# A hybrid state-space / RWKV block on one core: buffers and load order at the seam to the recurrence, and state-space steps ordered behind dense sums

## The chip, the cores and the metric

The kernel runs on one core of a Trainium2 chip. The metric is the device time of one execution in microseconds (us). Engines are named as in the profile: PE is TensorE, DVE VectorE, ACT ScalarE, POOL GpSimd, SP SyncE, which here only issues transfers. A core has all five, each with its own queue of instructions that it works off strictly in order.

## The reference, cut to what matters

One layer of a sequence model: 2048 positions, width 1024, all in float32.

```
h = RMSNorm(x);  [u | rwkv_in | gate_a | gate_b] = h @ W_in         # 512 | 1792 | 1024 | 1024 columns
o_a = S5(u):     x_t = A x_(t-1) + B u_t  (complex, diagonal, 32 groups x 64 states);  y = C x + D u;  gelu, half-GLU
o_b = RWKV7(p):  pm = p + (shifted p - p) * mu
                 r, k, v = pm columns;  decay, a from two low-rank products;  g from a third
                 S_t = S_(t-1) * w_t + (S_(t-1) a_t) b_t + v_t k_t ;   y_t = S_t r_t     (8 heads x 64)
merged = sigmoid(gate_a) * (o_a @ Wb_a) + sigmoid(gate_b) * (o_b @ Wb_b)
x = x + merged @ W_out;  x = x + relu(RMSNorm(x) @ W1)^2 @ W2;  out = RMSNorm(x)
```

## The kernel before

The program has four phases, traced one after the other: `phase_a` (norm, input projection, state-space branch), `phase_b` (RWKV recurrence with the gate products in its gaps), `phase_c` (half-GLU, branch and output products) and the feed-forward product. Float32 accuracy comes from splits: each operand is held as a high and a low part, and a product is three matmuls (`mm3`, lines 121 to 123: high weight by low input, low by high, high by high). A *group* is one 128x512 output tile in one PSUM bank: 8 slices of the inner dimension, 24 matmuls.

**The order of instructions** is not the order of the program text. A planner traces the program, simulates it with its own costs, and lets each engine issue what it takes to be ready first, earlier-traced instructions first among those. `tc.keep_in_program_order` (in the code often wrapped as `pin`) binds an instruction behind the one traced just before it on its engine, and only that one. A DMA counts as an instruction of the engine that issues it. Once fixed, each queue is worked off in order, so an instruction that waits holds up all behind it. Generators are woven at trace time: `weave(main, other, ratio=2)` takes two steps of `other` for each `yield` of `main`; `robin` takes one of each in turn.

**Phase A, the dense products** (`dense`, lines 527 to 575). The normalised input lies in SBUF as four tiles of 32 KB per partition: `hh0`, `hl0` (high and low part of windows 0 and 1) and `hh1`, `hl1` (windows 2 and 3). There are 14 weight tiles m in the order 17, 16, 4 ... 15, each with four windows w: 56 groups. After a group ScalarE writes `sg` from the PSUM bank, scaled by `om` (line 557); then VectorE adds the shifted part, the *dense sum* (line 558), adds the column carried from the window before (line 561) and copies the group's last column (line 565). That copy is the last reader of the bank; four banks turn. The tile `sg` (three buffers, shared with the low-rank results) is stored to `pm_d` by SP (line 572). For m = 17, `low_rank` multiplies by small matrices (line 591, two banks at once) and stores the sigmoids (lines 594, 596).

**Phase A, the state-space branch** (`s5_stream`) is woven into the dense groups at ratio 2; `dense` yields twice a group, so four state-space yields fall to one group. The 32 groups are done in 8 passes q. A pass multiplies the input by E (`px`, pinned on TensorE), copies to X, runs 12 *steps* on VectorE (`step`, lines 377 to 383: two multiplications into m1 and m2, two additions), spreads the carries (lines 397 to 403: two multiplications, two additions, for each of two state groups), makes the tables of the next pass (`prep`) and multiplies by F and TZ (`py`, pinned on TensorE). The last pass has no `prep` behind its steps.

**Phase B.** Its pools are opened anew over phase A's memory, and a tile waits for the tiles that lay at its place. From the tile sizes and the order in which the pools are opened: the constants' pool `b_c`, the gate pools `b_w` and `b_t` are stacked at the upper end. The constants `cstb` come first in `b_c` and lie partly over the last 4 KB of `hl1`; the first gate-weight buffer (in `b_w`) lies over the state-space tiles TZ0 and TZ1; the second (in `b_t`) lies over `om` and the last raw weight tile. The recurrence's inputs (pool `b_x`: rm, km, vm, sgx, sig, aa) lie within `hh0`.

The recurrence runs over 16 pieces of 128 positions. `elem(s)` makes the decays and scaled keys of a piece on VectorE, ScalarE and GpSimd (first step line 689, from km), `inv(s)` inverts the in-chunk matrices, `chain(s)` carries the state. At line 1027 `robin` turns between `chain(i-2)`, the gates `gg`, `elem(i)` and `inv(i-1)`. `gates` (from line 957) multiplies the 16 gate-weight tiles by the four windows of h, 64 groups: `raww` loads a raw weight tile, `loadw` splits it (ScalarE cast line 976, GpSimd subtraction line 977) and for the first window stores the split to `gs_d` (line 981). The window's input comes back from `h_d` as eight tiles gh0 to gh7 (`h{k}`): gh0 to gh4 in `b_w`, loaded by GpSimd's queue in the first window, gh5 to gh7 in `b_t`, loaded by SP.

Of the kernel before, what the change touches and what calls it, by code (L numbers as in the profile page):

```python
# [10 lines left out]
F32 = mybir.dt.float32  # L11
F32R = mybir.dt.float32r
# [3 lines left out]
ALU = mybir.AluOpType  # L16
# [5 lines left out]
NK = DM // 128  # L22
# [21 lines left out]
NCST_A = 144  # L44
# [217 lines left out]
def s5_stream(tc, nc, K, io, R, u_d, z_d, pool, ps):  # L262

    NP = 2
    V = nc.vector
# [4 lines left out]
    PW, PR, A8, NI, qr, qi = R.PW, R.PR, R.A8, R.NI, R.qr, R.qi  # L270
# [91 lines left out]
    for q in range(NQ):  # L362
        p0, f0 = q * NP, q * fw
# [10 lines left out]
        m1 = pool.tile([128, 2, NP, 32], F32, tag="m1", name=f"m1{q}")  # L374
        m2 = pool.tile([128, 2, NP, 32], F32, tag="m2", name=f"m2{q}")

        def step(dst, src, k, n):
            shp = [128, 2, NP, n]
            d1, d2 = m1[:, :, :, 0:n], m2[:, :, :, 0:n]
            V.tensor_tensor(d1, src, A8[:, 0:1, k, p0:p0 + NP].unsqueeze(3).to_broadcast(shp), op=ALU.mult)  # L380
            V.tensor_tensor(d2, src[:, ::-1], NI[:, :, k, p0:p0 + NP].unsqueeze(3).to_broadcast(shp), op=ALU.mult)
            V.tensor_tensor(d1, d1, d2, op=ALU.add)
            V.tensor_tensor(dst, dst, d1, op=ALU.add)

# [3 lines left out]
        for j in range(5):  # L388
            n = 32 - (1 << j)
            step(XB[:, :, :, 32 - n:32, 7], XB[:, :, :, 0:n, 7], 7 + j, n)  # L390
            yield
        for g in range(NP):
            shp = [128, 2, 31, 7]
            f1 = pool.tile([128, 2, 31, 7], F32, tag="f1", name=f"f1{q}_{g}")
            f2 = pool.tile([128, 2, 31, 7], F32, tag="f2", name=f"f2{q}_{g}")
            car = XB[:, :, g, 0:31, 7:8]
            V.tensor_tensor(f1, A8[:, 0:1, 0:7, p0 + g].unsqueeze(2).to_broadcast(shp), car.to_broadcast(shp), op=ALU.mult)
            V.tensor_tensor(f2, NI[:, :, 0:7, p0 + g].unsqueeze(2).to_broadcast(shp), car[:, ::-1].to_broadcast(shp),
                            op=ALU.mult)
            yield  # L400
            V.tensor_tensor(f1, f1, f2, op=ALU.add)
            dst = XB[:, :, g, 1:32, 0:7]
            V.tensor_tensor(dst, dst, f1, op=ALU.add)
            yield
# [22 lines left out]
def phase_a(tc, nc, K, io, u_d, pm_d, h_d, z_d):  # L427
    with ExitStack() as st:
# [11 lines left out]
        R = Net()  # L440
# [69 lines left out]
        mu = K.vec("mu_rwkv")  # L510
# [16 lines left out]
        def dense():  # L527
# [4 lines left out]
            for gi, (m, w) in enumerate(groups):  # L532
# [13 lines left out]
                i = m - 4  # L546
                pp = psm.tile([128, 512], F32, tag="mm", name=f"p{m}_{w}")
                o = 512 * (w % 2)
                for k in range(NK):
# [4 lines left out]
                    if side and k in (2, 6):  # L554
                        side.pop(0)()
                sg = wp.tile([128, 512], F32, tag="sg", name=f"sg{m}_{w}", bufs=3)
                nc.scalar.activation(sg, pp, ACTF.Copy, scale=om[:, i:i + 1])
                nc.vector.scalar_tensor_tensor(sg[:, 1:512], pp[:, 0:511], mu[:, i:i + 1], sg[:, 1:512],
                                               op0=ALU.mult, op1=ALU.add)
                if w:  # L560
                    nc.vector.scalar_tensor_tensor(sg[:, 0:1], lasts[m], mu[:, i:i + 1], sg[:, 0:1],
                                                   op0=ALU.mult, op1=ALU.add)
# [48 lines left out]
def phase_b(tc, nc, K, io, pm_d, ob_d, h_d, gt_d, gs_d, inv_d):  # L611
    V, A, P, T = nc.vector, nc.scalar, nc.gpsimd, nc.tensor
    NS = S // 128
    with ExitStack() as st:
# [8 lines left out]
        psi = st.enter_context(tc.tile_pool(name="b_pi", bufs=2, space=PSUM, reuse_waits="tile"))  # L623
        psc = st.enter_context(tc.tile_pool(name="b_pc", bufs=1, space=PSUM, reuse_waits="tile"))
        psy = st.enter_context(tc.tile_pool(name="b_py", bufs=1, space=PSUM, reuse_waits="tile"))
        ct = cp.tile([128, NCST - NCST_A], F32, name="cstb")
        cq = tc.keep_in_program_order(nc.gpsimd.dma_start(ct, io["cst"][:, NCST_A:]))

        def cst(n):
            o, w = COFF[n]  # L630
# [17 lines left out]
        eend = cp.tile([128, 4, 2 * NS + 1], F32, name="eend")  # L648
        gam = cp.tile([128, 4, 2 * NS + 1], F32, name="gam")
        P.memset(eend, 0.0)  # L650
        SB = [cp.tile([128, 4, 128], F32, name=f"SB{i}") for i in range(2)]
        for t in SB:
            P.memset(t, 0.0)

        def gps(n):
            return psg.tile([128, 512], F32, tag="g", name=n)

        D = [dict() for _ in range(NS)]

        def load(s, q=nc.sync):  # L660
            d = D[s]
            for i, n in enumerate(("rm", "km", "vm")):
                d[n] = xp.tile([128, 4, 128], F32, tag=n, name=f"{n}{s}", bufs=3 if n == "vm" else 2)
                (pin(q.dma_start) if s == 0 and n != "vm" else q.dma_start)(d[n], pm_d[512 * i:512 * i + 512, 128 * s:128 * s + 128].rearrange(
                    "(h p) t -> p h t", p=128))
            d["sgx"] = xp.tile([128, 128], F32, tag="sgx", name=f"sgx{s}", bufs=4)
            q.dma_start(d["sgx"], pm_d[1536:1664, 128 * s:128 * s + 128])
            for i, n in enumerate(("sig", "aa")):
                d[n] = xp.tile([128, 4, 128], F32, tag=n, name=f"{n}{s}", bufs=2)
                q.dma_start(d[n], pm_d[1664 + 512 * i:2176 + 512 * i, 128 * s:128 * s + 128].rearrange(  # L670
                    "(h p) t -> p h t", p=128))

        def fl(a):
            return a.rearrange("p h t -> p (h t)")

        def pin(f):
            return lambda *a, **k: tc.keep_in_program_order(f(*a, **k))

        def elem(s):
            d = D[s]  # L680
# [276 lines left out]
        def gates():  # L957
            late, keep = Late(), Late()

            def raww(m, q=nc.sync):  # L960
                wr = (gw, gt)[m % 2].tile([128, NK, 128], F32, tag="wr", name=f"gwr{m}")
                pin(q.dma_start)(wr, io["win"][18 + m])
                return wr

            def loadw(m, wr=None):

                pool = (gw, gt)[m % 2]
                wh = pool.tile([128, NK, 128], F32R, tag="wh", name=f"gwh{m}")
# [7 lines left out]
                A.copy(wh, wr)  # L976
                P.tensor_tensor(wl, wr, wh, op=ALU.subtract)  # L977

                def store():
                    for e, t in enumerate((wh, wl)):  # L980
                        nc.sync.dma_start(gs_d[m, e], t.bitcast(F32))

                keep.put(store)
                return wh, wl

            wr0 = raww(0, nc.gpsimd)
            yield
            wr1 = raww(1)
            for w in range(NW):
                hs = []  # L990
                for k in range(NK):
                    t = (gw if k < 5 else gt).tile([128, 2, 512], F32R, tag=f"h{k}", name=f"gh{w}_{k}")
                    q = nc.sync if w or k >= 5 else nc.gpsimd
                    (q.dma_start if w else pin(q.dma_start))(
                        t.bitcast(F32), h_d[:, w, :, k, :].rearrange("i p t -> p i t"))
                    r = t[:, 0], t[:, 1]
                    hs.append(r)
                if w == 0:
                    nxt = loadw(0, wr0)
                for _ in range(5):  # L1000
                    yield
                for m in range(16):
                    wh, wl = nxt
                    j = 16 * w + m
                    if j == 15:
                        keep.flush()
                    if j + 1 < 16 * NW:
                        nxt = loadw(j + 1, None if j else wr1)
# [10 lines left out]
            late.flush()  # L1019

        gg = Side(gates())
        next(gg)
        load(0, nc.gpsimd)
        next(gg)
        A.copy(bor, bo)
        for i in range(NS + 2):
            robin(chain(i - 2) if i >= 2 else None, gg, elem(i) if i < NS else None,
                  inv(i - 1) if 0 <= i - 1 < NS else None)
# [862 lines left out]
```

## Time and profile before

| what | value |
|---|---|
| median of 3 runs (lowest to highest) | 3067.3 us (3063.57 to 3067.74) |
| the profiled execution's own time | 3067.71 us |
| span in that profile, first to last instruction | 3065.8 us |
| mean granted TensorE clock | 0.975 |
| TensorE busy | 2915.4 us, 95% |
| VectorE busy | 1897.8 us, 62% |
| ScalarE busy | 1121.4 us, 37% |
| GpSimd busy | 1234.7 us, 40% |
| last dense matmul issued; dense products end | 539.97 us |
| first gate matmul | 550.17 us |

A row of the instructions in order of time reads: start in us, duration in us, engine, line, operation, output <- inputs, shapes, count; in brackets the idle time of the engine before it and what ended it. SPq is SP's queue. In the stretches each engine has its busy time and instruction count, then come the granted clock (1.00 is full), the DMA engines' busy share and GB/s. In the rows of DMA issues the last number is the median time from issue to landing.

### The profile page before, as it was taken

To read this page: it belongs to the slowest core of one execution; us is meant where nothing else is said; L and a number is where in the kernel's file an instruction comes from. 1 tells how busy PE (TensorE), PEld (TensorE's weight loads), DVE (VectorE), ACT (ScalarE), POOL (GpSimd) and SP (SyncE) were. 2 spreads that over 40 slices of the span, in tenths; PEclk is the share of its full clock that TensorE was granted. 3 is DMA by queue.
4 is the path that set the end of the run, shared out by engine and by line. 5 is a ranking of instruction groups with operands and counts; after the bars stand their busy time and mean duration, and the time that the engine had idled before them with its cause. 6 is when DMAs were issued, how large, how long until landed. Compare 5 with 4: busy or idle time off the path is not lost.

```text
span 3065.8 us, 45565 instructions
## 1 busy us (share of the span) xinstructions
PE 2915.4 (95%) x17024; PEld 2329.5 (76%) x17024; DVE 1897.8 (62%) x3307; ACT 1121.4 (37%) x1797; POOL 1234.7 (40%) x1082
## 2 busy tenths in 40 slices
PE   8989999689999999999999989999999999999998
PEld 6757777467777777777878778887788788888886
DVE  6366885467777677535322376658655476666667
ACT  5342111234333333234444365555433432222232
POOL 3101101754443343113333345555544565555563
PEclk9999999789999999999999999999999999999999
DMA  4344444755656455367665653333533486666664
GB/s 154 96 132 148 132 148 133 255 187 176 187 167 207 120 149 181 118 195 229 194 213 166 192 188 124 110 110 114 169 113 107 134 240 151 151 151 151 153 146 148
DMA packets 328172, 486.04 MB, mean 159 GB/s; under 512 B 112832, under 2 KB 171712, under 8 KB 327952
## 3 DMA queue, kind: packets, MB, share of 16 engines
q1 hardware_dynamic: 298352, 438.08, 44.8%
q0 software_dynamic: 12960, 40.87, 7.3%
q10 hardware_dynamic: 16640, 4.20, 0.5%
q8 instruction: 134, 2.20, 0.3%
q14 instruction: 86, 0.70, 0.1%
HBM read 327.71 MB, written 147.85 MB: 155 GB/s over the span
## 4 chain that ended last, share of the span: by engine, by line
PE 55%; DVE 10%; DMA 6%; issue 4%; POOL 3%; ACT 2%; SPq 1%; POOLq 0%; DVEq 0%; ACTq 0%
PE s L121 6%; PE s L122 6%; PE s L123 6%; PE f L121 6%; PE f L123 6%; PE f L122 6%; PE gp L121 2%; PE gp L122 2%; PE gp L123 2%; DMA g<-gt_d 1%; PE o L121 1%; DVE yt L813 1%; PE o L122 1%; DVE YC L815 1%; PE o L123 1%
## 5 line engine op out<-in xcount | busy, mean ns | idle before, releaser
L121 PE MATMUL f<-bl,w1h 128*128 128x512 f32 x896 | 354.4, 396 | 9.4 <-ACT w1h L1378 9.3
L122 PE MATMUL f<-bh,w1l 128*128 128x512 f32 x896 | 350.7, 391 | 5.1 <-POOL w1l L1382 5.1
L123 PE MATMUL f<-bh,w1h 128*128 128x512 f32 x896 | 352.1, 393 | 0.0
L121 PE MATMUL s<-w2l,ah 128*128 128x512 f32 x784 | 305.8, 390 | 2.9 <-ACT s L1619 2.9
L122 PE MATMUL s<-w2h,al 128*128 128x512 f32 x784 | 305.7, 390 | 0.0
L123 PE MATMUL s<-w2h,ah 128*128 128x512 f32 x784 | 305.6, 390 | 0.0
L1382 POOL TENSOR_TENSOR w1l<-w1r,w1h 128x512 fp32r<-128x512 f32 x122 | 179.9, 1478 | 180.2 <-ACT w1h L1378 179.8
L121 PE MATMUL gp<-gh,gwh 128*128 128x512 f32 x512 | 225.8, 441 | 21.4 <-ACT gwh L976 14.9
L122 PE MATMUL gp<-gh,gwl 128*128 128x512 f32 x512 | 211.6, 413 | 12.5 <-POOL gwl L977 11.7
L1378 ACT CAST w1h<-w1r 128x512 fp32r<-128x512 f32 x224 | 137.9, 620 | 207.9 <-PE f L123 149.7
L1596 POOL TENSOR_TENSOR al<-ra,ah 128x1024 fp32r<-128x1024 f32 x64 | 168.4, 2634 | 109.2 <-ACT ah L1595 109.0
L123 PE MATMUL gp<-gh,gwh 128*128 128x512 f32 x512 | 209.3, 409 | 0.0
L1626 DVE TENSOR_TENSOR c<-c,s 128x512 f32<-128x512 f32 x224 | 149.9, 684 | 90.5 <-PE s L123 89.8
L121 PEld LDWEIGHTS f<-bl,w1h 128*128 128x128 f32 x896 | 169.4, 189 | 45.7 <-ACT w1h L1378 10.9
L122 PEld LDWEIGHTS f<-bh,w1l 128*128 128x128 f32 x896 | 169.1, 189 | 44.6 <-POOL w1l L1382 7.9
L123 PEld LDWEIGHTS f<-bh,w1h 128*128 128x128 f32 x896 | 168.9, 188 | 38.3
L121 PE MATMUL p<-hl,wh 128*128 128x512 f32 x448 | 183.1, 409 | 0.2
L122 PE MATMUL p<-hh,wl 128*128 128x512 f32 x448 | 178.7, 399 | 0.0
L123 PE MATMUL p<-hh,wh 128*128 128x512 f32 x448 | 178.2, 398 | 0.0
L121 PEld LDWEIGHTS s<-w2l,ah 128*128 128x128 f32 x784 | 147.5, 188 | 33.9 <-ACT s L1619 3.3
L123 PEld LDWEIGHTS s<-w2h,ah 128*128 128x128 f32 x784 | 147.6, 188 | 30.9
L122 PEld LDWEIGHTS s<-w2h,al 128*128 128x128 f32 x784 | 147.5, 188 | 30.6
(392 smaller groups left out, 6778.7 us busy)
## 6 DMA issues: line engine op xcount, KB each, us to landing
w1r<-in_w_dram SPq DMA_DIRECT2D x64, 512.0 KB, 3.5
r_d<-c SPq DMA_DIRECT2D x128, 256.0 KB, 2.0
ra<-r_d SPq DMA_DIRECT2D x64, 512.0 KB, 3.5
gwl<-gs_d SPq DMA_DIRECT2D x48, 512.0 KB, 4.5
gwh<-gs_d SPq DMA_DIRECT2D x48, 512.0 KB, 4.8
ch<-r_d POOLq DMA_DIRECT2D x42, 512.0 KB, 5.7
gt_d<-gs SPq DMA_DIRECT2D x64, 256.0 KB, 5.0
g<-gt_d SPq DMA_DIRECT2D x64, 256.0 KB, 3.4
```

The costliest lines, as they stand in the source:

```text
L121: nc.tensor.matmul(ps, wh, xl, start=start, stop=False)
L122: nc.tensor.matmul(ps, wl, xh, start=False, stop=False)
L123: nc.tensor.matmul(ps, wh, xh, start=False, stop=stop)
L813: V.tensor_tensor(tv, NC[:, 0:k, k:k + 1].to_broadcast([64, k, n]), YC[:, k:k + 1, k:16].to_broadcast([64, k, n]), op=ALU.mult)
L815: V.tensor_tensor(YC[:, 0:k, k:16], YC[:, 0:k, k:16], tv, op=ALU.add)
L1378: cast = A.copy(h, o)
L1382: (P if n % 2 or edge else V).tensor_tensor(l, o, h, op=ALU.subtract)
L1596: P.tensor_tensor(l, raw[n], h, op=ALU.subtract)
L1626: V.tensor_tensor(d, d, bank, op=ALU.add if i in (4, 5, 6) else ALU.subtract)
```

## The change

Five edits, none of which changes what is computed.

1. In `s5_stream`, the two multiplications of every step and of every carry block are bound behind the latest dense sum that was traced before them (`R.last`, line 558); `tc.issue_after` adds an order on VectorE and no wait for completion. The multiplications into f1 and f2 (lines 397 and 398) are wrapped in the same way as those of `step`.
2. In `b_c`, the two state buffers SB are made first and the constants after them, so that the constants lie 4 KB higher. SB's memsets are traced later, just before the loop.
3. Both raw gate-weight buffers are now in `b_w` (tags wr0 and wr1). In exchange gh4 moves from `b_w` to `b_t`, to the place over `om`, and from GpSimd's queue to SP's.
4. The first loads are pinned in a new order, all on GpSimd's queue: gate weights 0, constants, then km, sig, aa, rm, vm, sgx of piece 0, gate weights 1, then gh0 to gh3. Before, only gate weights 0, constants, rm, km and gh0 to gh4 were pinned there, and gate weights 1 were on SP's queue. Later pieces are loaded in the new order on SP, not pinned.
5. Raw gate weights from the third on are no longer pinned; the stores of split weights are.

```diff
+        def behind():
+            return tc.issue_after(R.last.ins) if getattr(R, "last", None) else ExitStack()
         def step(dst, src, k, n):
...
-            V.tensor_tensor(d1, src, A8[:, 0:1, k, p0:p0 + NP].unsqueeze(3).to_broadcast(shp), op=ALU.mult)
-            V.tensor_tensor(d2, src[:, ::-1], NI[:, :, k, p0:p0 + NP].unsqueeze(3).to_broadcast(shp), op=ALU.mult)
+            with behind():
+                V.tensor_tensor(d1, src, A8[:, 0:1, k, p0:p0 + NP].unsqueeze(3).to_broadcast(shp), op=ALU.mult)
+                V.tensor_tensor(d2, src[:, ::-1], NI[:, :, k, p0:p0 + NP].unsqueeze(3).to_broadcast(shp), op=ALU.mult)
...
-                nc.vector.scalar_tensor_tensor(sg[:, 1:512], pp[:, 0:511], mu[:, i:i + 1], sg[:, 1:512],
+                R.last = nc.vector.scalar_tensor_tensor(sg[:, 1:512], pp[:, 0:511], mu[:, i:i + 1], sg[:, 1:512],
...
+        SB = [cp.tile([128, 4, 128], F32, name=f"SB{i}") for i in range(2)]
+        def raww(m, q=nc.sync):
+            wr = gw.tile([128, NK, 128], F32, tag=f"wr{m % 2}", name=f"gwr{m}")
+            (q.dma_start if m > 1 else pin(q.dma_start))(wr, io["win"][18 + m])
+            return wr
+        wr01 = [raww(0, nc.gpsimd)]
         ct = cp.tile([128, NCST - NCST_A], F32, name="cstb")
-        cq = tc.keep_in_program_order(nc.gpsimd.dma_start(ct, io["cst"][:, NCST_A:]))
+        pin(nc.gpsimd.dma_start)(ct, io["cst"][:, NCST_A:])
...
-        SB = [cp.tile([128, 4, 128], F32, name=f"SB{i}") for i in range(2)]
-        for t in SB:
-            P.memset(t, 0.0)
-        def load(s, q=nc.sync):
+        def load(s, q=None):
...
-            for i, n in enumerate(("rm", "km", "vm")):
-                d[n] = xp.tile([128, 4, 128], F32, tag=n, name=f"{n}{s}", bufs=3 if n == "vm" else 2)
-                (pin(q.dma_start) if s == 0 and n != "vm" else q.dma_start)(d[n], pm_d[512 * i:512 * i + 512, 128 * s:128 * s + 128].rearrange(
-                    "(h p) t -> p h t", p=128))
...
+            def get(n, src, bufs, shape=(128, 4, 128)):
+                d[n] = xp.tile(list(shape), F32, tag=n, name=f"{n}{s}", bufs=bufs)
+                (pin(q.dma_start) if q else nc.sync.dma_start)(d[n], src)
+            get("km", block(512), 2)
+            get("sig", block(1664), 2)
+            get("aa", block(2176), 2)
+            get("rm", block(0), 2)
+            get("vm", block(1024), 3)
+            get("sgx", pm_d[1536:1664, 128 * s:128 * s + 128], 4, (128, 128))
...
-            def raww(m, q=nc.sync):
-                wr = (gw, gt)[m % 2].tile([128, NK, 128], F32, tag="wr", name=f"gwr{m}")
-                pin(q.dma_start)(wr, io["win"][18 + m])
-                return wr
...
-                        nc.sync.dma_start(gs_d[m, e], t.bitcast(F32))
+                        pin(nc.sync.dma_start)(gs_d[m, e], t.bitcast(F32))
...
-            wr0 = raww(0, nc.gpsimd)
-            yield
-            wr1 = raww(1)
-                    t = (gw if k < 5 else gt).tile([128, 2, 512], F32R, tag=f"h{k}", name=f"gh{w}_{k}")
-                    q = nc.sync if w or k >= 5 else nc.gpsimd
+                    t = (gw if k < 4 else gt).tile([128, 2, 512], F32R, tag=f"h{k}", name=f"gh{w}_{k}")
+                    q = nc.sync if w or k >= 4 else nc.gpsimd
...
         gg = Side(gates())
-        next(gg)
         load(0, nc.gpsimd)
+        wr01.append(raww(1, nc.gpsimd))
         next(gg)
         A.copy(bor, bo)
+        for t in SB:
+            P.memset(t, 0.0)
```

More of the change, by code (lines that the diff above doesn't have):

```diff
@@ L396, in s5_stream @@
             car = XB[:, :, g, 0:31, 7:8]
-            V.tensor_tensor(f1, A8[:, 0:1, 0:7, p0 + g].unsqueeze(2).to_broadcast(shp), car.to_broadcast(shp), op=ALU.mult)
-            V.tensor_tensor(f2, NI[:, :, 0:7, p0 + g].unsqueeze(2).to_broadcast(shp), car[:, ::-1].to_broadcast(shp),
-                            op=ALU.mult)
+            with behind():
+                V.tensor_tensor(f1, A8[:, 0:1, 0:7, p0 + g].unsqueeze(2).to_broadcast(shp), car.to_broadcast(shp),
+                                op=ALU.mult)
+                V.tensor_tensor(f2, NI[:, :, 0:7, p0 + g].unsqueeze(2).to_broadcast(shp),
+                                car[:, ::-1].to_broadcast(shp), op=ALU.mult)
             yield
@@ L557, in dense @@
                 nc.scalar.activation(sg, pp, ACTF.Copy, scale=om[:, i:i + 1])
-                nc.vector.scalar_tensor_tensor(sg[:, 1:512], pp[:, 0:511], mu[:, i:i + 1], sg[:, 1:512],
-                                               op0=ALU.mult, op1=ALU.add)
+                R.last = nc.vector.scalar_tensor_tensor(sg[:, 1:512], pp[:, 0:511], mu[:, i:i + 1], sg[:, 1:512],
+                                                        op0=ALU.mult, op1=ALU.add)
                 if w:
@@ L625, in phase_b, with pin @@
         psy = st.enter_context(tc.tile_pool(name="b_py", bufs=1, space=PSUM, reuse_waits="tile"))
+        SB = [cp.tile([128, 4, 128], F32, name=f"SB{i}") for i in range(2)]
+        def pin(f):
+            return lambda *a, **k: tc.keep_in_program_order(f(*a, **k))
+        def raww(m, q=nc.sync):
[3 more added lines that the diff above has]
+        wr01 = [raww(0, nc.gpsimd)]
         ct = cp.tile([128, NCST - NCST_A], F32, name="cstb")
-        cq = tc.keep_in_program_order(nc.gpsimd.dma_start(ct, io["cst"][:, NCST_A:]))
+        pin(nc.gpsimd.dma_start)(ct, io["cst"][:, NCST_A:])
         def cst(n):
@@ L658, in phase_b, with block @@
         D = [dict() for _ in range(NS)]
-        def load(s, q=nc.sync):
+        def load(s, q=None):
             d = D[s]
-            for i, n in enumerate(("rm", "km", "vm")):
-                d[n] = xp.tile([128, 4, 128], F32, tag=n, name=f"{n}{s}", bufs=3 if n == "vm" else 2)
-                (pin(q.dma_start) if s == 0 and n != "vm" else q.dma_start)(d[n], pm_d[512 * i:512 * i + 512, 128 * s:128 * s + 128].rearrange(
-                    "(h p) t -> p h t", p=128))
[L666 to L671, printed above, removed]
+            def get(n, src, bufs, shape=(128, 4, 128)):
+                d[n] = xp.tile(list(shape), F32, tag=n, name=f"{n}{s}", bufs=bufs)
+                (pin(q.dma_start) if q else nc.sync.dma_start)(d[n], src)
+            def block(r0):
+                return pm_d[r0:r0 + 512, 128 * s:128 * s + 128].rearrange("(h p) t -> p h t", p=128)
+            get("km", block(512), 2)
[4 more added lines that the diff above has]
+            get("sgx", pm_d[1536:1664, 128 * s:128 * s + 128], 4, (128, 128))
         def fl(a):
             return a.rearrange("p h t -> p (h t)")
-        def pin(f):
-            return lambda *a, **k: tc.keep_in_program_order(f(*a, **k))
         def elem(s):
@@ L998, in gates @@
                 if w == 0:
-                    nxt = loadw(0, wr0)
+                    nxt = loadw(0, wr01[0])
                 for _ in range(5):
@@ L1007, in gates @@
                     if j + 1 < 16 * NW:
-                        nxt = loadw(j + 1, None if j else wr1)
+                        nxt = loadw(j + 1, None if j else wr01[1])
                     pp = psd.tile([128, 512], F32, tag="d", name=f"gp{j}")
```

## The prediction

> **What bounds the kernel now.** I read the stretches of 25 us first (busy time, granted clock and DMA share by stretch), then who waited for whom on TensorE, then the instructions in order of time around the two places where TensorE stands still. The page's head says that TensorE is the bound:
>
> ```profile
> span 3065.8 us, 45565 instructions
> PE 2915.4 (95%) x17024; PEld 2329.5 (76%) x17024; DVE 1897.8 (62%) x3307; ACT 1121.4 (37%) x1797; POOL 1234.7 (40%) x1082
> ```
>
> So a change pays only where it removes TensorE idleness, or the half clock behind it. The answer for chosen stretches (busy us of PE, PEld, DVE, ACT, POOL; then granted clock, DMA share, GB/s) shows both places:
>
> ```profile
> 219.00:229.00 10.00, 0.00 (x0) 0.00 (x1) 9.41 (x27) 1.21 (x2) 0.00 (x0) 0.75 0.00 0
> 229.00:234.20 5.20, 5.17 (x15) 3.71 (x16) 2.72 (x4) 1.38 (x2) 0.00 (x0) 0.50 0.80 214
> 245.00:495.00 250.00, 250.00 (x1189) 194.38 (x1188) 190.29 (x469) 50.38 (x75) 25.46 (x28) 1.00 0.45 135
> 517.60:540.40 22.80, 22.76 (x98) 18.03 (x96) 2.79 (x9) 3.06 (x5) 3.95 (x6) 1.00 0.83 264
> 540.40:550.20 9.80, 0.03 (x1) 0.03 (x1) 2.10 (x3) 2.03 (x3) 6.33 (x12) 0.73 1.00 335
> 550.20:556.10 5.90, 0.76 (x1) 0.26 (x1) 1.97 (x1) 1.09 (x2) 2.34 (x1) 0.50 1.03 380
> 556.10:570.50 14.40, 14.36 (x50) 11.26 (x50) 1.50 (x3) 5.79 (x9) 14.37 (x23) 0.80 0.90 325
> 570.50:579.70 9.20, 0.00 (x0) 0.00 (x0) 4.99 (x8) 0.00 (x0) 7.65 (x10) 0.77 0.45 119
> 579.70:593.00 13.30, 9.66 (x27) 6.83 (x27) 13.18 (x13) 5.03 (x9) 11.38 (x12) 0.76 0.62 176
> 640.00:1345.00 705.00, 663.38 (x6987) 514.81 (x6986) 480.19 (x972) 232.96 (x401) 251.32 (x326) 0.97 0.54 164
> ```
>
> **Place one**, 219 to 229 us, in the dense products: TensorE idle 10 us with VectorE 94% busy, then 5.2 us at clock 0.50. **Place two**, the seam from the dense products to the recurrence: 9.8 us idle, one matmul, 5 us idle, two gate groups, 9.2 us idle. From 245 to 495 TensorE never stops, and there nothing can be won. At place one:
>
> ```profile
> 214.04 0.69 ACT L557 ACTIVATE sg<-p,om 128x512 f32<-128x512 f32 x1
> 213.93 0.41 DVE L380 TENSOR_TENSOR m<-X,A 128x128 f32<-128x128 f32 x1
> 215.47 0.40 DVE L380 TENSOR_TENSOR m<-X,A 128x128 f32<-128x128 f32 x1
> 227.94 0.74 DVE L558 SCALAR_TENSOR_TENSOR sg<-p,vec,sg 128x511 f32<-128x511 f32 x1
> 228.73 0.15 DVE L565 COPY lc<-p 128x1 f32<-128x1 f32 x1
> 229.03 0.79 PE L591 MATMUL lr<-xl,lrh 64*128 64x512 f32 x2 [10.17 <-DVE lc L565]
> 218.94 1.27 ACT L594 ACTIVATE lo<-lr,vec 128x512 f32<-128x512 f32 x2 [4.21 <-PE lr L591]
> ```
>
> A dense group's sum (L558) could start when ScalarE ends at 214.73. VectorE starts it at 227.94: the planner put state-space steps (L380 and on) in front. The group's last-column copy (L565) frees the PSUM bank for which the low-rank product waits.
>
> **Part 1: the tie.** The two multiplications of each step, and of each carry block, may not be issued before the last dense sum traced. No instruction is added. By the trace order (four state-space yields to a dense group), only steps traced before a sum may still precede it, and when the sum is ready it also comes earlier in the program. A step is four operations, 1.54 us (from one L380 to the next above). At 214.73 one step is running, so the sum would run at 215 to 217. The bank is then free at about 217. The other bank of that low-rank pair is freed by the sigmoids of L594, done at 218.94 + 1.27 = 220.2, so I let TensorE resume there instead of at 229.03: 8.8 us. The 5.2 us at clock 0.50 cost 2.6 and fall away with the long wait. Together **-11.4, taken as -11**. Bounds: -12.8 (10.17 + 2.6, no wait left) and -4 (the next low-rank pair meets the three-buffer ring of stores).
>
> What waits behind a tied step? The step chain itself, and for its end the pinned products py. In steady state:
>
> ```profile
> 373.05 0.69 ACT L557 ACTIVATE sg<-p,om 128x512 f32<-128x512 f32 x1 [4.86 <-PE p L123]
> 379.07 0.61 DVE L403 TENSOR_TENSOR X<-X,f 128x434 f32<-128x434 f32 x1
> 380.45 0.74 DVE L558 SCALAR_TENSOR_TENSOR sg<-p,vec,sg 128x511 f32<-128x511 f32 x1
> 385.47 1.13 PE L268 MATMUL py<-X,F 64*128 64x256 f32 x8
> 510.39 0.61 DVE L403 TENSOR_TENSOR X<-X,f 128x434 f32<-128x434 f32 x1
> 511.05 1.22 PE L268 MATMUL py<-X,F 64*128 64x256 f32 x4 [2.08 <-DVE X L403]
> ```
>
> The state is ready at 379.7 and py starts at 385.5: 5.8 us of slack. Sums that now run behind the chain (this one is 6.7 us late) go in front of it, 0.74 and two tiny ones, 1.1 us each; with two of them the chain ends 2.2 us later, inside the slack, so it costs 0. Without that cover it would be 2.2 us for each of the seven earlier groups. The last group has no preparation behind it and no slack: py already waits 2.08. One sum in front makes **+1** (0 to +3, if two sums and half clock go with it).
>
> **Part 2: the seam.** The rows in the order of the chain:
>
> ```profile
> 516.22 1.75 PE L268 MATMUL py<-uT,TZ 128*128 128x256 f32 x4
> 529.48 0.80 POOL L667 DMA_DIRECT2D sgx<-pm_d  x1 [28.47 <-PE p L123]
> 540.20 0.55 POOL L627 DMA_DIRECT2D cstb<-in_cst_dram  x1 [6.97 <-PE p L122]
> 541.84 0.55 POOL L677 DMA_DIRECT2D gwr<-in_win_dram  x1
> 543.12 0.77 POOL L677 DMA_DIRECT2D km<-pm_d  x1
> 543.45 1.19 SPq L677 DMA_DIRECT2D gwr<-in_win_dram  x1
> 550.17 0.79 PE L121 MATMUL gp<-gh,gwh 128*128 128x512 f32 x1 [9.81 <-ACT gwh L976]
> 551.12 1.97 DVE L689 TENSOR_TENSOR kr<-km,vec 128x512 f32<-128x512 f32 x1 [2.66 <-DMA km<-pm_d]
> 556.10 0.80 PE L121 MATMUL gp<-gh,gwh 128*128 128x512 f32 x1 [5.14 <-ACT gwh L976]
> 579.71 0.80 PE L122 MATMUL gp<-gh,gwl 128*128 128x512 f32 x1 [9.25 <-POOL gwl L977]
> 593.03 2.07 PE L677 MATMUL m<-AR,BK 64*128 64x128 f32 x14 [3.66 <-DVE bv L757]
> 540.40 0.69 ACT L557 ACTIVATE sg<-p,om 128x512 f32<-128x512 f32 x1 [4.87 <-PE p L123]
> km<-pm_d POOLq DMA_DIRECT2D x1, 256.0 KB, 8.0
> gh<-h_d POOLq DMA_DIRECT2D x5, 512.0 KB, 10.1
> gh<-h_d SPq DMA_DIRECT2D x3, 512.0 KB, 14.6
> ```
>
> The constants (cstb) lie over the last piece of the second half's low part, so their load waits for the last dense group (540.20), and the first gate weights and km, pinned behind them, wait as well. The second gate weights lie over om, which ScalarE reads until 541.1. Tile sizes and pool order say where these go: the two state buffers SB take the low end of the pool; cstb moves 4 KB up, over state-space tiles last read by py (518); both gate-weight buffers sit over state-space tiles whose last reader is py or the store behind it. All inputs of the recurrence (xp) lie over the first half's high part, free at 529.5, as sgx's row shows.
>
> GpSimd's queue becomes: gate weights 0 and cstb at about 518, then from 529.5 km, sig, aa, rm, vm, sgx, gate weights 1, gh0 to gh3, at 0.55 to 0.80 us each. km goes 13.6 us earlier (543.12 to 529.5), so kr can start at 529.5 + 8.0 = 537.5. If VectorE has the last dense sum queued in front (ready at 541.1), it is 542. Against 551.12 that is -9 to -13.6 for the element chain. gh0 is the eighth of these: 529.5 + 7 x 0.75 = 534.7, plus 10.1 is 544.8. By then both weights are split, so TensorE restarts at 545, not 550/556: -11 against 556.10.
>
> What is late next: gh4. It moves from GpSimd's queue to SP's, and its place (the gate pool's low end) lies over om, so it and the pinned gh5 to gh7 go out at 541.1 and land 8.0 to 14.6 later, 549 to 555.7. The first group's second half, 12 matmuls of a 24-matmul group, waits for them. Two groups take 11.2 us (48 matmuls at 22.8 / 98 = 0.233), so they end between 559 and 564 instead of 570.5: -6.5 to -11.5. After that, splits and element steps on GpSimd set the pace (14.37 busy of 14.40), and they start 9 to 13.6 earlier. I take **-11** for the seam, between these: **bounds -5 and -16**.
>
> The rest costs nothing beside running work: the two SB memsets now wait for 540.4 and are first read a round later; the gate-weight stores pinned on SP hold up only loads that are a group ahead; raw loads unpinned from the third on may go earlier. In the 705 us stage behind, however, the planner deals all queues anew: TensorE idles 705 - 663.4 = 41.6 us there, and I allow a quarter, 10 us, either way.
>
> The clock rows: after idle of 10 us and of 9.2 us TensorE ran some 5 to 6 us at 0.50. In the Trainium skill, "TensorE: Matmul & The Clock Gate", section "What's actually happening", says that an idle window of about 3.4 us throttles to half, and as long a busy one releases it. By it a seam wait of 545 - 540.4 = 4.6 us would still throttle, for 2.6 us by the row from 229; the seam's bounds hold that. The trace agrees: 0.75 in the idle stretch from 219, 0.50 behind it.
>
> **Sum**: -11 + 1 - 11 = -21 against the profiled execution's 3067.71 us (span 3065.8, 1.9 around it), which lies 0.4 above the median 3067.3: **3047**.
>
> **The rivals.** (a) *The seam is bound by bandwidth.* For: DMA share 1.00 and 1.03 from 540 to 556. Loads issued earlier then mostly share the same engines, and gh4 to gh7 land at 555.7: seam -4, sum -14, 3054. Against: 517.6 to 540.4 has free bytes. At 380 GB/s in place of 264 it could move 2.6 MB more; weights 0, cstb and five inputs are 512 + 672 + 5 x 256 KB, 2.5 MB. The Trainium skill's "DMA: Bandwidth & Descriptors", section "Issuing engines are not separate DMA queues", speaks for (a): queues share 16 engines, so a changed queue saves issue time alone. This trace agrees in so far as two queues together stop at 380 GB/s.
>
> (b) *The seam flows through.* The 9.25 us wait for a split queued behind km's update, and the 3.66 for bv, come from queue order; with elements ahead of the gates they vanish with 3 us of half clock: another -15, 3032. Against: GpSimd stays the stage's busiest engine.
>
> (c) *Slower: the chain of steps falls behind.* If tied steps stand idle for sums (a sum is ready only after its group and 0.69 on ScalarE), the state comes late for py, in each of seven groups. It costs from 5.8 us of lateness on. At 10 us: 4.2 x 7 = 29, plus 2.6 of half clock each, 18; less 21: +26, 3094. Against: steps already need more VectorE time than the dense groups give, so they rarely wait.
>
> (d) *No effect:* the planner keeps the hoist or the recurrence stage gives the gain back (-21 + 10 + 5 by the bounds): 3062 to 3070, say 3066.
>
> **How the numbers follow.** Forecast 0.42 (own range 3038 to 3056), (a) 0.18, (b) 0.17, (c) 0.09, (d) 0.14. Faster by over 0.2% (6.1 us, about what can be told from no change) is below 3061: forecast, (a), (b): 0.77. (d) gives same 0.14, (c) slower 0.09. The range leaves out (c) and the lower part of (b): 3022 to 3068.
>
> **What would show it.** In the changed profile: no wait of a low-rank product for lc above 2 us, and dense sums within 3 us of ScalarE's end; py waits at the last group only; cstb's issue near 518, km's near 529.5; the first gate matmul near 545, and the second half of the first group waiting for gh. Waits for py in all groups would prove me wrong, as would a cstb issue that still stands behind 540.

## The result, and the profile after

| | before | changed |
|---|---|---|
| median, us | 3067.52 (4 runs, 3063.57 to 3069.61) | 3046.28 (4 runs, 3045.68 to 3048.03) |
| ratio, 95% interval | | 0.9933 [0.9916, 0.995] |
| profiled execution, us (span) | 3067.71 (3065.8) | 3045.86 (3043.9) |

Faster, by 21.9 us in the profiled executions and 21.2 in the medians, where 21 were predicted. A second measurement (e9), beside other kernels, gave 0.9937 [0.992, 0.9954].

> The changed kernel once more, beside the next three on the same chip. Theory: 0.9933 of the kernel before, as first measured, and what the tie alone (0.9975) and the seam alone (0.9962) give together (0.9937): within 0.992 to 0.995. Rival (the first measurement of 4 runs was a lucky one): above 0.995.

The changed kernel's page, its head, and then the answer for chosen stretches (busy us of PE, PEld, DVE, ACT, POOL; granted clock, DMA share, GB/s):

```profile
span 3043.9 us, 45570 instructions
PE 2908.1 (96%) x17024; PEld 2323.0 (76%) x17024; DVE 1900.6 (62%) x3307; ACT 1123.0 (37%) x1797; POOL 1231.1 (40%) x1082
```

```profile
219.00:229.00 10.00, 9.41 (x45) 6.80 (x44) 6.61 (x21) 3.73 (x6) 0.00 (x0) 1.00 0.56 165
245.00:495.00 250.00, 250.00 (x1180) 194.54 (x1179) 191.19 (x473) 50.06 (x75) 26.39 (x25) 1.00 0.44 134
495.00:517.00 22.00, 16.34 (x62) 11.17 (x61) 10.04 (x23) 1.77 (x3) 1.60 (x4) 0.77 0.72 243
533.80:545.60 11.80, 4.95 (x13) 3.42 (x13) 5.53 (x6) 5.81 (x8) 7.48 (x8) 0.82 1.05 371
545.60:563.90 18.30, 14.78 (x49) 10.49 (x49) 8.16 (x7) 4.63 (x8) 17.57 (x25) 0.84 0.95 354
620.00:1325.00 705.00, 668.00 (x7054) 520.40 (x7053) 479.48 (x977) 233.65 (x402) 257.37 (x334) 0.98 0.55 167
```

The hole at 219 us is gone, and the clock there is 1.00. The middle of the dense products is full, as before. A new hole stands at 495 to 517, at clock 0.77. In the seam the DMA engines are full (1.05, 0.95). The recurrence idles 37.0 us in 705, before 41.6.

Place one, in order of time:

```profile
215.98 0.69 ACT L564 ACTIVATE sg<-p,om 128x512 f32<-128x512 f32 x1
216.70 0.75 DVE L565 SCALAR_TENSOR_TENSOR sg<-p,vec,sg 128x511 f32<-128x511 f32 x1
217.49 0.15 DVE L572 COPY lc<-p 128x1 f32<-128x1 f32 x1
221.24 0.50 PE L598 MATMUL lr<-xl,lrh 64*128 64x512 f32 x1 [0.59 <-ACT lo L601]
```

The sum runs 0.03 us after ScalarE ends; before, it ran 13.2 us after. The low-rank product waits 0.59 us, for the sigmoids. ScalarE writes `sg` of the sixteenth dense group (L564, before L557) at 258.1 and not 268.2, and up to the fifty-second group this lead stays between 10.06 and 10.13 us.

The last pass, in order of time:

```profile
472.46 0.59 ACT L371 COPY X<-px 128x512 f32<-128x512 f32 x1 [0.28 <-PE px L268]
475.49 0.69 ACT L564 ACTIVATE sg<-p,om 128x512 f32<-128x512 f32 x1 [2.44 <-DMA z_d<-uT]
476.21 0.75 DVE L565 SCALAR_TENSOR_TENSOR sg<-p,vec,sg 128x511 f32<-128x511 f32 x1 [10.51 <-ACT sg L564]
477.00 0.38 DVE L385 TENSOR_TENSOR m<-X,A 128x128 f32<-128x128 f32 x1
501.90 1.23 PE L268 MATMUL py<-X,F 64*128 64x256 f32 x4 [4.10 <-DVE X L410]
504.68 1.22 PE L268 MATMUL py<-X,F 64*128 64x256 f32 x4 [1.56 <-DVE X L410]
533.35 0.40 PE L123 MATMUL p<-hh,wh 128*128 128x512 f32 x1
```

The state is loaded at 473.05. The first step is tied behind a sum that is ready at 476.2, and starts at 477.00, 3.95 us late: VectorE stood still for 3.16 us and then ran the sum. In the kernel before, it started 0.03 us after the state. py waits 4.10 and 1.56 us (before 0.35 and 2.08), and 3.5 of the 10.1 us are gone: the dense products end 6.6 us earlier.

The seam:

```profile
512.46 0.56 POOL L636 DMA_DIRECT2D cstb<-in_cst_dram  x1
522.84 0.78 POOL L636 DMA_DIRECT2D km<-pm_d  x1 [9.57 <-PE p L123]
535.29 0.68 DVE L705 TENSOR_TENSOR kr<-km,vec 128x512 f32<-128x512 f32 x1
535.45 0.50 PE L121 MATMUL gp<-gh,gwh 128*128 128x512 f32 x1 [1.71 <-ACT gwh L987]
538.29 0.79 PE L121 MATMUL gp<-gh,gwh 128*128 128x512 f32 x1 [2.34 <-ACT gwh L987]
541.74 2.36 POOL L988 TENSOR_TENSOR gwl<-gwr,gwh 128x1024 fp32r<-128x1024 f32 x1 [2.63 <-DMA pm_d<-sg]
544.04 0.19 POOL L719 COPY cmid<-e 128x8 f32<-128x8 f32 x1
545.62 0.79 PE L121 MATMUL gp<-gh,gwh 128*128 128x512 f32 x1 [2.89 <-DMA gh<-h_d]
559.59 0.50 PE L122 MATMUL gp<-gh,gwl 128*128 128x512 f32 x1 [2.02 <-POOL gwl L988]
563.93 1.74 DVE L752 RECIPROCAL sq<-n 128x256 f32<-128x256 f32 x1
1330.54 0.39 PE L123 MATMUL gp<-gh,gwh 128*128 128x512 f32 x1
```

cstb no longer waits for the last dense product, km is issued 10.5 us ahead of it, and TensorE restarts within 2.1 us of it (before, 10.2). The first reciprocals, by which I mark the seam's end, come at 563.9 (before 580.5).

All kernels in one table, profiled executions, us. A: start of the last dense product. B: from there to the first reciprocals. C: from there to the last gate product. D: the rest of the span, whose code the diff does not touch. They are differences of rounded times and can be off by 0.1.

| kernel | A | B | C | D | median against before |
|---|---|---|---|---|---|
| before | 540.0 | 40.5 | 768.5 | 1716.8 | 1 |
| changed | 533.4 | 30.5 | 766.6 | 1713.4 | 0.9933 |
| e9, changed again | 534.1 | 28.5 | 763.8 | 1711.6 | 0.9937 |
| e1, tie alone | 533.5 | 39.1 | 769.6 | 1712.3 | 0.9975 |
| e2, seam alone | 536.8 | 27.6 | 772.1 | 1710.0 | 0.9962 |
| e3, last pass free | 528.1 | 27.9 | 768.5 | 1715.8 | 0.9936 |
| e4, places, old loads | 531.6 | 34.4 | 799.0 | 1707.1 | 1.0046 |
| e5, e3 and vm last | 528.6 | 24.2 | 775.1 | 1711.6 | 0.9933 |
| e6, e3 and split later | 530.2 | 24.0 | 796.4 | 1710.3 | 1.0001 |
| e8, old order | 532.4 | 29.7 | 760.3 | 1709.7 | 0.9928 |
| e10, raw loads pinned | 534.3 | 30.3 | 770.2 | 1712.8 | 0.994 |
| e11, order, old places | 533.2 | 44.0 | 772.7 | 1714.6 | 1.001 |
| e12, e8 and e3 | 529.1 | 33.9 | 765.0 | 1716.5 | 0.991 |
| e13, longer chain | 536.3 | 27.9 | 765.7 | 1712.2 | 0.9947 |

D ranges over 10 us with code that no edit touches, so of the 21.9 us the 3.4 in D cannot be put down to the change: a single profile tells A and B, and the medians the rest. The kernel before had 3062 to 3064 as its median beside e1 to e13, hence ratios only.

### The profile page after: what moved, and what is told of

Read it like the earlier page. It is cut to its first block, busy times and chain, and to the rows that moved or that the text cites. A ratio compares the mean times of both kernels' runs of the same rounds, so it can differ in the third digit from the quotient of the medians.

```text
span 3043.9 us, 45570 instructions
## 1 busy us (share of the span) xinstructions
PE 2908.1 (96%) x17024; PEld 2323.0 (76%) x17024; DVE 1900.6 (62%) x3307; ACT 1123.0 (37%) x1797; POOL 1231.1 (40%) x1082
## 4 chain that ended last, share of the span: by engine, by line
PE 56%; DVE 10%; DMA 6%; issue 3%; POOL 3%; ACT 2%; SPq 1%; POOLq 0%; DVEq 0%; ACTq 0%
PE s L122 6%; PE s L123 6%; PE s L121 6%; PE f L121 5%; PE f L123 5%; PE f L122 5%; PE gp L121 3%; PE gp L122 2%; PE gp L123 2%; DMA g<-gt_d 2%; DMA wor<-in_wout_dram 1%; DVE YC L831 1%; DVE yt L829 1%; PE U L923 1%; DVE bl L1361 1%
## 5 line engine op out<-in xcount | busy, mean ns | idle before, releaser
L123 PEld LDWEIGHTS s<-w2h,ah 128*128 128x128 f32 x784 | 147.2, 188 | 30.5
```

The costliest lines, as they stand in the source:

```text
L123: nc.tensor.matmul(ps, wh, xh, start=False, stop=stop)
```

## The experiments

**The two parts apart: e1, e2.** e1 is the kernel before with `behind()` and `R.last`; e2 is the changed kernel without them.

> The kernel before with the tie alone. Theory (the two parts add): the dense groups start 10.1 us earlier from the eleventh group on, the last pass of the chain gives 3.5 back because its first step stands idle for a tied sum, and nothing else moves: the last dense group ends 6.6 us earlier, and the time is 3067.5 - 6.6 = 3061. Rival (the tie helps the seam too, since sums that run early let the first element steps start): more than 6.6, down to 3055. Rival (the seam eats the gain, because its loads are bound by bandwidth and not by when the dense products end): 3067.

> The changed kernel without the tie, so the seam's part alone. Theory: TensorE's 10.2 us wait at 219 us is back, the last pass waits for the state about 2.4 us as before, the last dense group ends at 540 as before, and the seam still gains 10 us by the first reciprocals and about 12 by the recurrence's end: 3052 to 3056. Rival (loads that need the time the tie made free): a seam gain of under 5, 3060 or more. If the 3.4 us that the changed kernel won behind the recurrence come from the seam's part, the time is at the low end; if they are only another deal of the planner, they are not here.

Measured: e1 0.9975 [0.9965, 0.9985], 7.7 us of 3062.8, near the theory's 6.6; e2 0.9962 [0.9947, 0.9977], 11.6 us, at the edge of the theory's 11.5 to 15.5. Together 19.3, against 19.3 (0.9937) and 20.6 (0.9933) of the whole change: within these intervals, 3 to 5 us to either side, the parts add. TensorE's waits in e1, then in e2:

```profile
503.25 1.23 PE L268 MATMUL py<-X,F 64*128 64x256 f32 x4 [4.09 <-DVE X L410]
543.52 0.80 PE L121 MATMUL gp<-gh,gwh 128*128 128x512 f32 x1 [9.58 <-ACT gwh L983]
548.15 0.80 PE L121 MATMUL gp<-gh,gwh 128*128 128x512 f32 x1 [3.84 <-ACT gwh L983]
571.77 0.80 PE L122 MATMUL gp<-gh,gwl 128*128 128x512 f32 x1 [9.23 <-POOL gwl L984]
```

```profile
226.75 0.80 PE L591 MATMUL lr<-xl,lrh 64*128 64x512 f32 x2 [10.13 <-DVE lc L565]
544.94 1.19 PE L121 MATMUL gp<-gh,gwh 128*128 128x512 f32 x2 [7.73 <-DMA gh<-h_d]
553.52 0.50 PE L121 MATMUL gp<-gh,gwh 128*128 128x512 f32 x1 [2.29 <-DMA gh<-h_d]
```

With the tie alone the seam's three waits are nearly those of before (9.81, 5.14, 9.25), 6.6 to 8 us earlier. With the seam alone the 10 us at place one are back. The tie moves the dense end by 6.4 us against the profile of before, by 3.3 against e2's. e2's dense products, of the same code as those of before, ended at 536.8 and not at 540 as I had expected: they were 1.7 us ahead at the sixteenth group, and had the clock at 0.92 around the last pass, where before had 0.86.

**The tail: e3, e5, e6.** e3 leaves the last pass untied:

```
-            return tc.issue_after(R.last.ins) if getattr(R, "last", None) else ExitStack()
+            return tc.issue_after(R.last.ins) if getattr(R, "last", None) and q + 1 < NQ else ExitStack()
```

> The changed kernel with the tie in all passes of the state-space chain but the last. Theory (the first tied step waits idle for the sum that it is tied behind, about 4 us, and only the last pass has no slack for it): py waits 0.4 and 2.1 us as in the kernel before, the wait at 219 us stays away, the last dense group ends 10.1 us earlier than before and not 6.6, and the time is 3046.3 - 3.5 = 3042.8. Rival (the last pass is late for the sums that run ahead of its steps in any case): 3045 to 3047. Rival (the seam's loads are bound by bandwidth, so an earlier end of the dense products only lengthens the wait): 3046.

Measured 0.9936 [0.9923, 0.9949]. The step's theory holds and the time's does not. TensorE, GpSimd and VectorE in e3:

```profile
500.63 0.74 PE L268 MATMUL py<-X,F 64*128 64x256 f32 x4 [2.08 <-DVE X L410]
526.97 0.75 POOL L636 DMA_DIRECT2D vm<-pm_d  x1 [6.36 <-DMA pm_d<-sg]
528.78 2.84 POOL L636 DMA_DIRECT2D gh<-h_d  x4
535.90 1.19 PE L121 MATMUL gp<-gh,gwh 128*128 128x512 f32 x2 [7.40 <-DMA gh<-h_d]
555.97 1.74 DVE L752 RECIPROCAL sq<-n 128x256 f32<-128x256 f32 x1
```

The dense products end at 528.1, 5.3 us before the changed kernel's, but gates start at 535.9, where they started at 535.45: vm's load waits for the store of a dense sum, and the gate weights and gh are pinned behind it. The element chain does come 8.0 us earlier. A 95% interval of 0.0026 is 8 us wide, so whether some 3 us came through cannot be told. The gates end at 1324.5, 6.1 us before the changed kernel's and 1.9 before e9's.

e5 loads vm and sgx last, e6 delays the second gate split so that GpSimd copies cmid first; both stand on e3 (in e5 `load` leaves vm and sgx of block 0 to a function `rest`):

```
         wr01.append(raww(1, nc.gpsimd))
         next(gg)
+        rest()                                # e5: vm and sgx of block 0
...
-                for _ in range(5):
+                for _ in range(5 if w else 7):    # e6
```

> The kernel whose last pass is free of the tie, and in it the loads of vm and sgx pinned behind the second gate weights and gh0 to gh3, not ahead of them. Theory (with the last pass free, vm's issue waits 6.4 us for the store of a dense sum, and the gate weights and gh, pinned behind it, are late by that; TensorE's 7.4 us wait for gh follows from it): gh0 is issued by 523 and not at 528.8, TensorE starts the gates within 3 us of the last dense product, and the time is 3 to 6 us under that of the kernel whose last pass is free, so about 0.992. Rival (bandwidth: the 16 engines are 0.89 to 1.07 busy from 520 to 560, so gh lands as late as before whatever its place, or takes the time from the inputs of the element chain): the same or up to 5 us more, 0.9935 to 0.995.

> The kernel whose last pass is free of the tie, and in it the second gate group's split traced two rounds later, so that GpSimd copies cmid ahead of it. Theory (cmid is ready 3.7 us before GpSimd copies it, since GpSimd stands at the split of the second gate weights, whose place is still being read by a store; the element chain sets the seam's end): the first reciprocals come about 3 us earlier than 556.0 and the time falls by 2 to 4, to about 0.9925. Rival (TensorE is kept by the gates and loses there what the elements win, as the split comes later): the same, 0.9936, or slower.

Measured: e5 0.9933 [0.9919, 0.9948], e6 1.0001 [0.999, 1.0011]. Each moves the seam the way it says, by less than I had expected. In e5 gh is issued at 526.28 (I had expected 523), the gates start at 532.5, 3.9 us behind the last dense product (I had expected 3), and B falls to 24.2; in e6 cmid is copied at 536.75, 4.4 us earlier than in e3, but the reciprocals gain 1.7. Both lose it behind. e5:

```profile
576.05 0.79 PE L636 MATMUL m<-AR,BK 64*128 64x128 f32 x2 [8.04 <-DVE TM L807]
613.33 2.07 PE L636 MATMUL m<-AR,BK 64*128 64x128 f32 x14 [5.44 <-DVE bv L779]
```

In e5 the first norm of the recurrence (its y reciprocal) comes at 652.9, in e3 at 641.5. In e6, C is 28 us longer than in e3. Neither theory nor rival had this size: the stage is dealt anew by each edit. What in e6's deal costs 28 us was not taken apart.

**Which part of the seam's edit pays: e4, e8, e10, e11.** e4 keeps the new places but takes back the load function, with its order and pins, and the second gate weights' queue; its weight stores stay pinned, and its raw loads are pinned as well:

```
-        wr01.append(raww(1, nc.gpsimd))
+        wr01.append(raww(1))
-            get("km", block(512), 2)
...
+            for i, n in enumerate(("rm", "km", "vm")):
+                (pin(q.dma_start) if s == 0 and n != "vm" else q.dma_start)(d[n], ...)
```

> The changed kernel with the first loads in the old order and the old pins (rm and km pinned, the others free, the second gate weights on SP), so only the tie and the places of the buffers. Theory (the places of cstb and of the gate weights made km late, the order adds little): km is issued by 526, the seam keeps at least 7 of its 10 us, 3046 to 3050. Rival (the order in which the loads are issued is what lets the element chain start early, since the loads share one bandwidth): the seam keeps less than 4 us, 3053 to 3060.

Measured 1.0046 [1.0033, 1.0059], 22 us slower than the tie alone by the ratios (19 by the medians). Against the kernel before, B is 6.1 us shorter (the changed kernel's is 10.0), and C is 30.5 longer. SyncE's queue, ScalarE and TensorE in e4:

```profile
529.00 0.59 SPq L636 DMA_DIRECT2D gwr<-in_win_dram  x1
544.67 1.04 ACT L983 CAST gwh<-gwr 128x1024 fp32r<-128x1024 f32 x1 [10.15 <-DMA gwr<-in_win_dram]
545.76 0.80 PE L121 MATMUL gp<-gh,gwh 128*128 128x512 f32 x1 [11.60 <-ACT gwh L983]
565.46 0.79 PE L122 MATMUL gp<-gh,gwl 128*128 128x512 f32 x1 [5.20 <-POOL gwl L984]
```

The second gate weights, issued at 529.0, can be split at 544.7 only: 15.7 us, while GpSimd's queue loads the inputs. The 6.1 us lie between theory (7 kept) and rival (under 4), and the time is above both. e8 and e10 each take one suspect of e4 into the changed kernel: the old order of the six tensors, and the pin of every raw load.

```
-            (q.dma_start if m > 1 else pin(q.dma_start))(wr, io["win"][18 + m])
+            pin(q.dma_start)(wr, io["win"][18 + m])
```

> The changed kernel with its inputs of each block loaded in the old order (rm, km, vm, sgx, sig, aa), all pins and places kept. Theory (the places and the pins made the gain, and kr starts behind the last dense sum anyhow): no more than 3 us slower than the changed kernel, 0.993 to 0.995. Rival (the order of use is what counts, as the kernel with the places alone, which had the old order and lost 19 us against the tie alone, suggests): 10 us slower or more, 0.997 and above.

> The changed kernel with the raw loads of all gate weights pinned on SP, as in the kernel before, and not only the first two. Theory (the places alone lost 29 us between the first reciprocals and the gates' end because raw loads and weight stores were both pinned there, so that each raw load stood behind the store of a split that was late): it loses 10 us or more, 0.997 or above. Rival (they lost it by the first loads: second gate weights 15 us under way, vm, sgx, sig and aa out of their order): as the changed kernel, 0.992 to 0.995.

Measured: e8 0.9928 [0.991, 0.9946], e10 0.994 [0.9924, 0.9955]: neither can be told from the changed kernel. So the order of use earns nothing that shows, and my theory for e10 falls. What is left of e4 is its unpinned first loads and the second weights on SyncE's queue; which of the two, or whether the suspects cost only together, and how C comes to lose 30 us from it, stays open.

e11 is the counterpart: tie, order and pins as changed, places as before, its second gate weights on GpSimd's queue.

> The kernel before with the tie and with the new order, pins and queues of the loads, but the old places (cstb over the second half's low part, the second gate weights over om). Theory (the places are what the seam needs: cstb is issued behind the last dense product, and all loads pinned behind it wait with it): cstb is issued at about the last dense product's end, km a few us behind it, the first reciprocals come no earlier than with the tie alone (39 us behind the last dense product), and the time is that of the tie alone or up to 8 us above, 0.9975 to 1.000. Rival (the order makes the gain without the places): 0.994 or below.

Measured 1.001 [0.9998, 1.0021], 11 us slower than the tie alone. GpSimd's queue and TensorE in e11:

```profile
533.47 0.80 POOL L634 DMA_DIRECT2D cstb<-in_cst_dram  x1 [42.97 <-PE p L122]
535.91 0.79 POOL L666 DMA_DIRECT2D km<-pm_d  x1
542.20 0.72 POOL L666 DMA_DIRECT2D gh<-h_d  x1 [1.45 <-DMA gwr<-in_win_dram]
543.83 0.73 POOL L666 DMA_DIRECT2D gh<-h_d  x1 [0.92 <-DMA km<-pm_d]
553.57 1.19 PE L121 MATMUL gp<-gh,gwh 128*128 128x512 f32 x2 [19.95 <-DMA gh<-h_d]
```

Everything pinned behind cstb waits with it for the last dense product, and TensorE idles 19.95 us. The pins without the places are a loss, and the places with e4's loads are one in time, though they keep 6.1 us in the seam: the gain in time needs both.

**e12** puts e3's and e8's edits together.

> The changed kernel with the old order of the tensors in each block's loads and with the last pass free of the tie: two edits that each moved the gates' end by some us in its profile, at a time that could not be told from the changed kernel's. Theory (they add: 4 to 6 us from the last pass, 2 to 4 from the order): the gates end 6 to 10 us earlier than in the changed kernel, about 1320, and the time is 0.990 to 0.9925. Rival (the recurrence is dealt anew and gives it back, as it did where vm went last): 0.993 to 0.996.

Measured 0.991 [0.989, 0.993], the lowest of all, in the theory's range. The interval overlaps the changed kernel's 0.9937 [0.992, 0.9954], and the profiled execution was the longest of its six (3046.67; 3028.1 to 3046.67) and ends the gates at 1328, not at 1320. So the theory's sign, the gates' end, did not come in the one profile. That it beats the changed kernel is not shown, since the lowest of a dozen medians is low partly by chance; where it would gain isn't shown either.

**The slack: e13.** In each pass, from the state's arrival to its last carry, and from there to py, the rows of the changed kernel give 31.1 to 33.7 us and 0.8 to 3.3 us of slack in the third to seventh pass. Before it was 27.4 to 28.5, and 5.8 to 7.0.

```
-                V.tensor_tensor(d1, src, A8[:, 0:1, k, ...
-                V.tensor_tensor(d2, src[:, ::-1], NI[:, :, k, ...
+                for _ in range(1 if k else 2):
+                    V.tensor_tensor(d1, src, A8[:, 0:1, k, ...
+                    V.tensor_tensor(d2, src[:, ::-1], NI[:, :, k, ...
```

> The changed kernel with the two multiplications of each of a pass's first seven state-space steps done twice (the result is the same), which makes each pass's chain 7 x 0.77 = 5.4 us longer. Theory (the tie has eaten the slack that the chain had: 0.8 to 3.3 us are left in six of the passes, where the kernel before had 5.8 to 7.0): py waits in seven of the eight passes, 2 to 5 us in each, 20 to 30 us in all with the half clock behind the longer waits: 0.999 to 1.004. Rival (VectorE's idle stretches before the sums take the longer chain in, so the tie cost no slack): under 8 us, below 0.9965.

Measured 0.9947 [0.993, 0.9965]: the rival's time, and in part its reason. All waits of py for the state in e13:

```profile
332.38 0.70 PE L268 MATMUL py<-X,F 64*128 64x256 f32 x4 [0.90 <-DVE X L411]
421.95 0.70 PE L268 MATMUL py<-X,F 64*128 64x256 f32 x4 [1.23 <-DVE X L411]
507.80 1.23 PE L268 MATMUL py<-X,F 64*128 64x256 f32 x4 [7.85 <-DVE X L411]
```

The slack is used up: between the state's end and the first py 0.1 us is left, or less than nothing, in passes two to seven. py did not give way: counted from the state's arrival it starts as in the changed kernel, to 0.02 us, in each of these passes. The chain grew by less than 5.4 us. The 14 added multiplications cost some 4.2 us of VectorE's time in a pass. In passes two, five and seven the chain is only 0.7 to 2.4 us longer, as VectorE's idle time within it fell by 1.8 to 3.1. In the third, fourth, sixth and last pass the idle time hardly moved, and the chain is 3.6 to 4.9 us longer. Even so only two waits, 2.1 us together, come of it before the last pass. The first four matmuls of py wait for the first state group's carry alone, and ran ahead of the last carry's end in passes three, four and six (330.78 against 332.33 in the fourth): the slack that I counted to the last carry was some 0.6 us too small. The last pass waits 7.85 us in one piece, for 4.10 and 1.56, but dense products then run before the next four matmuls; from the state's arrival to the last dense product it takes 61.1 us, for 60.3.

## Why the prediction was right, point by point

**Place one, -11: right.** The sum ran at 216.7 (215 to 217), TensorE resumed at 221.2 (220.2), for the sigmoids, as named; -10.1 in the pair of profiles, -7.0 between e1 and e2 (among tied kernels without e13, of equal code so far, the sixteenth group's row differs by up to 3.7 us). One sign did not come: I had expected all dense sums within 3 us of ScalarE's end, and 15 of 56 start later, by up to 6.23 us (before 21, up to 13.21). Up to four steps are traced between two sums and may still precede the second: four run from 404.76 to 409.95, 5.2 us. TensorE does not wait for these sums.

**Steady state, 0: right, with the wrong reason.** I counted two sums moved ahead, 2.2 us of 5.8. The chain became 3 to 6 us longer. In two of the five passes from the third on, its first step starts 4.0 us late, as in the last pass above; in the other three two more sums run in it; and in all five VectorE idles 3.2 to 5.8 us within it, where it idled 1.3 to 1.4. The argument "so they rarely wait", by which I put rival (c) at 0.09, is false. (c) did not come since the slack held, with 0.8 us left in the seventh pass: that was close. By e13 a longer chain is in part taken in by VectorE's idle time, so (c)'s price per late pass was too high.

**Tail, +1 with 0 to +3: mis-sized.** The step that failed is "one sum in front makes +1". The cost is not the sum's length alone, 1.1 us, but the idle wait for it as well: the first step starts 3.95 us late. It measured +3.5 in the pair, outside the bounds; 3.2 of them are py's longer waits (4.10 and 1.56, for 0.35 and 2.08). From ScalarE's row of the fifty-second group to the last dense product the tied kernels (without e13) take 34.3 to 35.7 us; e3, e5, e6 and e12, whose last pass is free, and e2 take 30.6: 3.7 to 5.1 us by kernels of equal code elsewhere. The kernel before, of e2's code there, took 32.0.

**Seam, -11, bounds -5 and -16: right.** It measured -10.0, -12.0 in e9, -11.5 between e2 and e1. With the dense end 6.6 us earlier, the predicted times shift by as much. km: 529.5 becomes 522.9, was 522.84. kr behind the last dense sum: 542 becomes 535.4, was 535.29. The second half of the first group waits for gh, 2.89 us. Only the restart came sooner than the shifted 538.4, at 535.45, as gh0 landed 7.4 us behind its issue (527.65 to 535.01) and not 10.1; then TensorE stopped twice.

**The re-deal, within 10 us: right here (-1.9, -4.7), too narrow as a rule.** Over all edits C runs from 760 to 799.

**The sum: partly luck.** Place one, tail, seam and re-deal measured -10.1, +3.5, -10.0 and -1.9, together -18.5. The profiled execution reached -21.9 by the 3.4 in D, which was not forecast and is within what D varies by; it makes up for a tail that cost 2.5 more than forecast and for some 1 us too little at place one and in the seam.

**Rivals.** (a) did not come. The DMA share is 1.05 behind the dense end, and of e3's 5 us nothing shows in its median, but e3's gates waited behind a load held up by a store, so that bandwidth limits the next step is not shown. (b): the wait for gwl fell from 9.25 to 2.02; the one for bv stayed, 3.87 us at 572.9, so the seam did not flow through. The argument against (b), that GpSimd stays the stage's busiest engine, holds for the seam (17.57 of 18.30 us); over the 705 us behind, VectorE is busier, 479 us to 257. (c) is answered above. (d) did not come.

## What to carry to other kernels

A tie that makes urgent work run first also makes the tied work wait for it, idle: read how late the first tied instruction starts, and try leaving the tie out where nothing lies behind the chain (in e3 the dense products then ended 5.3 us earlier, though its median shows no gain). Pinning loads in order pays only when the first pinned load has a place that is free early; with a late place it holds up the whole queue (e11). In a stage that a planner deals, an edit that does what it says in one place can lose far more behind it (e6, 28 us): judge by the stage's end.

## What the hardware showed beside

**VectorE stands beside GpSimd's split.** In the changed kernel (VectorE's scan, and GpSimd's split beside it):

```profile
535.49 2.70 POOL L988 TENSOR_TENSOR gwl<-gwr,gwh 128x1024 fp32r<-128x1024 f32 x1 [4.39 <-ACT gwh L987]
535.90 3.37 DVE L715 TENSOR_TENSOR_SCAN e<-cstb,sig 128x512 f32<-128x512 f32 x1
L715 DVE TENSOR_TENSOR_SCAN e<-cstb,sig x16: 1173/1216/3373, 535.9 to 1165.2; 128x512 f32<-128x512 f32 x16
```

The scan, 1.22 us in the median of its 16, took 3.37 and ended 1.1 us after the split: it seems to have started its work when the split was done. Over the 14 profiles 31 of these scans took more than 1.5 us, and each of them ended 1.07 to 1.10 us after the end of a GpSimd tensor operation. The Trainium skill, "SBUF — State Buffer", section "Who interferes with whom", names such a lock of the port pair that both share; this row agrees. The start of the scan moved 11.3 us forward, and 2.2 of them went into this.

The state-space chain pays the same price, which I had overlooked. From the third pass on, five step multiplications of the changed kernel take 1.7 to 2.5 us and not 0.4 (three in the kernel before), and each ends 0.08 to 0.18 us after a split of dense weights on GpSimd. In the last pass (its split ran from 488.39 to 490.78):

```profile
488.58 2.37 DVE L385 TENSOR_TENSOR m<-X,A 128x124 f32<-128x124 f32 x1
```

**GpSimd's queue had eight loads under way.** In e11 each gh waits for the landing of the load issued eight places before it (the first for the gate weights, the second for km). Whether chip or program sets this number was not tried.

**The clock.** Behind the 4.10 and 1.56 us waits of the last pass the clock is 0.50 from 500.4 to 510.6; beside the 0.59 us wait at place one it is 1.00. Behind waits of 0.35 and 2.08 us it is 0.50 from 510.7 to 517.5 in the kernel before, but only from 509.8 to 513.1 in e2, whose waits there are the same to 0.02 us. So less idle in one piece than the 3.4 us of the prediction was enough here, and the same waits do not always give as much half clock.
